# The down product of 1024 sample tokens as seven products over pairs of token tiles instead of eight

## The chip, the cores and the metric

One NeuronCore of a Trainium2 chip runs the whole program. The metric is device time in microseconds, from launch to the last output; runs of one kernel agree within about 0.3%. The trace of one profiled execution gives start, duration and wait of each instruction. Engines: TensorE (PE, with its weight loads as PEld), VectorE (DVE), ScalarE (ACT), GpSimd (POOL), SyncE (SP, which issues nearly all DMA transfers).

## What is computed

One layer of a diffusion transformer over 1024 sample tokens and 128 prompt tokens, in float32. The change touches only the last product, the down product of the feed-forward block:

```python
h = rmsnorm(x, P['g_pre_ffn'][l]) * (1.0 + sc2) + sh2
gt, up = jnp.split(h @ P['w_gate_up'][l], 2, axis=-1)
f = (jax.nn.silu(gt) * up) @ P['w_down'][l]        # (1152 x 2816) @ (2816 x 1024)
x = x + g2 * rmsnorm(f, P['g_post_ffn'][l])
```

## The kernel before

A float32 product is made of three PE passes: each operand is split into a high part (a copy by ACT into a rounded type, `copy`) and a low part (the difference, by DVE, `lo`), and `mm3` adds high x low, high x high and low x high. Every operand tile thus costs one ACT and one DVE instruction before PE can use it. `mm3` issues the two products with the high part of the stationary operand first.

The **gate and up stage** already uses seven products for eight: `VIS` lists 25 visits to the 22 hidden tiles g of 128 hidden units; each visit makes seven products (p = 0 to 6) for one or both chunks of tokens (c = 0: 640 tokens, c = 1: 512 tokens). Tokens of a tile of 128 are taken as two halves of 64. POOL makes the sums of weights (`weight_sums`), DVE combines the PSUM banks (`after`), and the hidden values `hf` go to HBM as `HB[tile, partition, j, token]`. The first three tiles g = 0, 1, 2 are visited for c = 0 alone and come back for c = 1 after g = 6, 10, 14. In the last visit c = 0 and c = 1 are done one after the other, so that loads for the next stage can begin between them.

The **down stage** has 18 runs `(n, t)`: two halves n of 512 output columns, nine token tiles t (tile 8 is the prompt). A run is 22 x 3 = 66 matmuls of 512 columns into one PSUM bank. Weights are loaded as 512 KB pieces (`load_d`, tile names raw_gu) and split into dw and gu tiles (`split_d`); the hidden tiles of a run are two halves of 11 (`load_h`, tile hr, 704 KB, two buffers; `split_h`, tile hd). In the second half the runs end with `post`: ACT squares the bank for the norm, DVE multiplies by the gain, POOL makes the reciprocal root (`rstd2`), DVE adds the residual `xr` twice, and SP stores the output tile `y`.

The order of the work on each engine is the order of the code (no scheduler moves anything). Each engine, SP included, takes its instructions in that order, and SP's are the issues of transfers: a transfer that waits, for a buffer or for data, is at the head of SP's queue, and what the code issues later comes behind it. ACT and DVE run ahead of PE as far as buffers and these orders allow; `post` of a run stands at j = 1 of the run after it.

Of the kernel before, what the change touches and what calls it, by code (L numbers as in the profile page):

```python
# [16 lines left out]
P = 128  # L17
D = 1024
# [3 lines left out]
NT = T // P  # L22
# [66 lines left out]
def _layout(inp):  # L89
    a = {k: np.asarray(v) for k, v in inp.items()}  # L90
    o = {}
# [15 lines left out]
    o["w_down"] = (a["w_down"][0].reshape(NJ // 2, 2, P, 2, 512).transpose(0, 3, 2, 1, 4)  # L107
                   .reshape(NJ, P, D))
# [44 lines left out]
def _body(tc, nc, A):  # L153
# [39 lines left out]
    ML = tc.dram_tile([D, T], F32, name="ML")  # L193
    X1 = tc.dram_tile([T, D], F32, name="X1")
    HB = tc.dram_tile([NT, P, NJ, P], F32, name="HB")
    H2B = tc.dram_tile([2, P, D], F32, name="H2B")
    GR = tc.dram_tile([2, 16, P], F32, name="GR")

# [1376 lines left out]

    dw, dstage = [], {}

    def load_d(i):  # L1580

        if i < NJ:
            r = (raw[1][:, 0], raw[1][:, 1], raw[0][:, 0])[i % 3]
            n, j = divmod(i, NJ // 2)
            dstage[i] = r
            SP.dma_start(r, A["w_down"][2 * j + n])

    def split_d(i):
        if i < 2 * NJ:
            r, w = dstage[i // 2][:, i % 2 * 512:i % 2 * 512 + 512], dw[i % len(dw)]  # L1590
            copy(ACT, w[:, 0], r)
            lo(w[:, 1], r, w[:, 0])
            if i % 2:
                load_d(i // 2 + 3)

    hid, hraw = {}, {}

    def load_h(t, i):

        r = hraw[t, i] = dp.tile([P, NJ // 2, P], F32, name=f"hr{t}{i}{len(hid)}", tag="hr", bufs=2)  # L1600
        SP.dma_start(r, HB[t, :, NJ // 2 * i:NJ // 2 * (i + 1)])

    def split_h(t, i):
        h = hid[t, i] = dp.tile([P, 2, NJ // 2, P], F32R, name=f"hd{t}{i}{len(hid)}", tag="hd", bufs=4)
        r = hraw.pop((t, i))
        copy(ACT, h[:, 0], r)
        lo(h[:, 1], r, h[:, 0])

    nprep = NS0
    extra = second_chunk()  # L1610
    H8 = 4
    for v, (g, cs) in enumerate(VIS):
        last = v == NV_ - 1
        for c_ in ([(c,) for c in cs] if last else [cs]):
            if last and c_ == (1,):
                avp.release()
                dp = pool("dp", side="right", reuse_waits="tile")
                load_h(0, 0)
                G2 = [dp.tile([P, D], F32, name="G2"), raw[0][:, 1]]
                fv = dp.tile([P, NT, 2], F32, name="fv")  # L1620
            for p in range(7):
                q = 7 * v + p
                while nprep <= q + LEADQ:
                    prep(nprep)
                    nprep += 1
                if q == 4:
                    op[0].release()
                    gb = pool("gb", space=PSUM, reuse_waits="tile")
                    banks += [4, 5]
                bs = [product(q, c) for c in c_]  # L1630
                if q in (H8, H8 + 1):
                    h2_turn(8, q - H8)
                    h2_mod(8, q - H8)
                if q == 13:
                    banks += [6, 7]
                after(q, c_, bs)
                if extra is not None and next(extra, 1):
                    extra = None
                if v == NV_ - 2 and p == 3:
                    load_d(0)  # L1640
                    load_d(1)
                if last and c_ == (0,):
                    if p == 0:
                        dw += [mo.tile([P, 2, 512], F32R, name=f"dw{i}", tag="tm" if i < 2 else "ou",
                                       bufs=2) for i in range(4)] + slots
                    if p == 3:
                        load_d(2)
                    if 1 <= p <= 4:
                        split_d(p - 1)
                elif last:  # L1650
                    if p == 1:
                        load_h(0, 1)
                    if p == 4:
                        split_h(0, 0)
                    if p > 0:
                        split_d(p + 3)
        if v == 2:
            assert extra is None

    fp.release()  # L1660
    dq = pool("dq", reuse_waits="tile")
    dw += [dq.tile([P, 2, 512], F32R, name=f"dw{i}") for i in range(len(dw), 24)]
    fg = [dq.tile([P, 512], F32, name=f"fg{t}") for t in range(NT)]
    xr = {}

    def load_x1(t):
        xr[t] = dp.tile([P, D], F32, name=f"xr{t}", tag="xr", bufs=2)
        SP.dma_start(xr[t], X1[t * P:(t + 1) * P])

    def post(t, n, b):  # L1670
        gt = G2[0 if t < 8 else 1][:, 512 * n:512 * n + 512]
        ACT.activation(t2, b, AF.Square, accum_out=fv[:, t, n:n + 1])  # L1672
        f = t3 if n else fg[t]
        DVE.tensor_tensor(f, b, gt, op=OP.mult)
        if n:
            rstd2(fv[:, t])
            x = xr[t].rearrange("p (n c) -> p n c", c=512)
            for i, y in enumerate((fg[t], t3)):
                DVE.scalar_tensor_tensor(x[:, i], y, fv[:, t, 0:1], x[:, i], op0=OP.mult, op1=OP.add)
                if t == 0:  # L1680
                    SP.dma_start(A["y"][t * P:(t + 1) * P, 512 * i:512 * i + 512], x[:, i])
            if t > 0:
                SP.dma_start(A["y"][t * P:(t + 1) * P], xr[t])

    runs = [(0, t) for t in range(NT)] + [(1, t) for t in reversed(range(NT))]
    done = None
    for i, (n, t) in enumerate(runs):
        nxt = None
        if n == 0 and t + 1 < NT:
            nxt = t + 1  # L1690
        elif n == 1 and 0 < t < NT - 1:
            nxt = t - 1
        b = bank(f"d{n}_{t}")
        for j in range(NJ):
            if i == 0 and j + 10 < NJ:
                split_d(j + 10)
            if j == 0:
                if nxt is not None and i:
                    load_h(nxt, 0)
                    load_h(nxt, 1)  # L1700
                if n:
                    load_x1(t)
            if i == 0 and j == 2:
                split_h(0, 1)
            if i == 0 and j in (6, 8):
                load_h(nxt, int(j > 6))
            if i == 0 and j == 11:
                grow(G2[0], 1, 0)
                grow(G2[1], 1, 1)
            if nxt is not None and j in ((14, 18) if i == 0 else (8, 14)):  # L1710
                split_h(nxt, int(j > 8 if i else j > 14))
            if j == 1 and done is not None:
                post(*done)
            if (n, t) == (0, 7) and j in (16, 18):
                split_d(NJ + (j - 16) // 2)
            h = hid[t, j // 11]
            w = dw[(NJ * n + j) % len(dw)]
            mm3(b, h[:, 0, j % 11], h[:, 1, j % 11], w[:, 0], w[:, 1], j == 0, j == NJ - 1)
            if (n, t) == (0, NT - 1) and j > 0:
                split_d(NJ + 2 + j - 1)  # L1720
        done = t, n, b
    post(*done)
    dp.release()
    mo.release()
    ring.release()
# [27 lines left out]
```

## Time and profile before

| what | value |
|---|---|
| median of 3 runs (lowest to highest) | 1435.22 us (1434.53 to 1440.06) |
| the profiled execution, its own time | 1430.3 us |
| its span, first to last instruction | 1428.5 us |
| its mean granted TensorE clock | 0.995 of full speed |
| PE, DVE, ACT, POOL busy, share of the span | 96%, 58%, 40%, 30% |

Busy shares are averages over stages that differ. PE's matmuls overlap in the pipeline, so that their listed durations (some 390 ns for 512 columns) are longer than the distance from one to the next. "SPq" rows are the issues of transfers by SP; a landing time runs from the issue to the end of the transfer.

### The profile page before, as it was taken

To read this page: it belongs to the slowest core of one execution; us is meant where nothing else is said; L and a number is where in the kernel's file an instruction comes from. 1 tells how busy PE (TensorE), PEld (TensorE's weight loads), DVE (VectorE), ACT (ScalarE), POOL (GpSimd) and SP (SyncE) were. 2 spreads that over 40 slices of the span, in tenths; PEclk is the share of its full clock that TensorE was granted. 3 is DMA by queue.
4 is the path that set the end of the run, shared out by engine and by line. 5 is a ranking of instruction groups with operands and counts; after the bars stand their busy time and mean duration, and the time that the engine had idled before them with its cause. 6 is when DMAs were issued, how large, how long until landed. Compare 5 with 4: busy or idle time off the path is not lost.

```text
span 1428.5 us, 22758 instructions
## 1 busy us (share of the span) xinstructions
PE 1375.9 (96%) x8918; PEld 1248.9 (87%) x8918; DVE 822.0 (58%) x1247; ACT 573.4 (40%) x1138; POOL 427.6 (30%) x426
## 2 busy tenths in 40 slices
PE   7899999998999999998999999999999989999998
PEld 6887799888889888887899999999999968888886
DVE  5724464564888843667866767667666653243232
ACT  6511136734888863555322323223222342142120
POOL 2301111222666662447634334333423100000000
PEclk9999999999999999999999999999999999999999
DMA  8558840147755335563222312222222472334541
GB/s 328 178 202 276 266 158 31 63 158 174 179 136 146 96 108 166 176 209 111 78 93 64 101 59 93 84 74 99 67 77 82 137 275 89 115 109 166 182 151 59
DMA packets 108326, 193.40 MB, mean 135 GB/s; under 512 B 7701, under 2 KB 77754, under 8 KB 104762
## 3 DMA queue, kind: packets, MB, share of 16 engines
q1 hardware_dynamic: 108074, 191.41, 41.7%
q8 instruction: 71, 1.16, 0.4%
q10 hardware_dynamic: 144, 0.52, 0.1%
q14 instruction: 37, 0.30, 0.1%
HBM read 146.67 MB, written 45.24 MB: 134 GB/s over the span
## 4 chain that ended last, share of the span: by engine, by line
PE 49%; DVE 2%; issue 1%; ACT 1%; DMA 1%; POOL 0%; DVEq 0%; POOLq 0%; SPq 0%; ACTq 0%
PE g L186 10%; PE g L184 10%; PE g L185 10%; PE d L186 6%; PE d L184 6%; PE d L185 6%; DVE gu L174 1%; DMA hr<-HB 1%; DVE av L174 0%; ACT gu L168 0%; DMA raw_gu<-in_w_down 0%; DVE u L1530 0%; DVE hf L1530 0%; DVE hd L174 0%; ACT av L168 0%
## 5 line engine op out<-in xcount | busy, mean ns | idle before, releaser
L186 PE MATMUL g<-av,gu 128*128 128x320 f32 (+1 forms) x1232 | 364.2, 296 | 7.7 <-DVE gu L174 7.3
L184 PE MATMUL g<-av,gu 128*128 128x320 f32 (+1 forms) x1232 | 364.3, 296 | 1.2 <-ACT av L168 0.8
L185 PE MATMUL g<-av,gu 128*128 128x320 f32 (+1 forms) x1232 | 363.1, 295 | 0.0
L186 PEld LDWEIGHTS g<-av,gu 128*128 128x128 f32 x1232 | 232.1, 188 | 10.3 <-DVE gu L174 10.2
L184 PEld LDWEIGHTS g<-av,gu 128*128 128x128 f32 x1232 | 231.9, 188 | 2.3 <-issue 1.4
L185 PEld LDWEIGHTS g<-av,gu 128*128 128x128 f32 x1232 | 232.2, 188 | 0.0
L174 DVE TENSOR_TENSOR gu<-raw_gu,gu 128x512 fp32r<-128x512 f32 x139 | 141.2, 1023 | 40.1 <-ACT gu L168 40.1
L184 PE MATMUL pu<-hl,w 128*128 128x384 f32 x336 | 123.0, 366 | 4.6 <-POOL hl L174 3.8
L186 PE MATMUL pu<-hh,w 128*128 128x384 f32 x336 | 113.1, 337 | 0.0
L185 PE MATMUL pu<-hh,w 128*128 128x384 f32 x336 | 113.1, 337 | 0.0
L184 PE MATMUL d<-dw,hd 128*128 128x512 f32 x270 | 106.7, 395 | 3.2 <-DVE dw L174 3.1
L186 PE MATMUL d<-dw,hd 128*128 128x512 f32 x270 | 106.4, 394 | 0.9 <-DVE hd L174 0.9
L185 PE MATMUL d<-dw,hd 128*128 128x512 f32 x270 | 106.4, 394 | 0.0
L1371 POOL TENSOR_TENSOR raw_gu<-raw_gu,t 128x512 f32<-128x512 f32 x25 | 33.2, 1329 | 233.4 <-DVE gu L174 233.4
L1530 DVE TENSOR_TENSOR u<-g,u 128x320 f32<-128x320 f32 (+1 forms) x176 | 77.5, 450 | 29.8 <-PE g L186 29.8
L940 PE MATMUL s<-ks,qs 128*128 128x384 f32 x384 | 91.0, 358 | 3.0 <-ACT p L953 1.5
L946 DVE TENSOR_REDUCE nm<-s 128x1 f32<-128x1152 f32 x64 | 86.6, 1353 | 9.4 <-PE s L940 9.2
L953 ACT ACTIVATE p<-s,nm 128x1152 f32<-128x1152 f32 x64 | 78.2, 1222 | 29.5 <-DVE nm L946 16.4
L1672 ACT ACTIVATE t<-d 128x512 f32<-128x512 f32 x18 | 10.7, 596 | 186.4 <-PE d L186 186.4
L168 ACT ACTIVATE gu<-raw_gu 128x512 fp32r<-128x512 f32 x139 | 83.4, 620 | 3.5 <-DMA raw_gu<-in_w_down 3.4
L1080 POOL TENSOR_SCALAR fv<-fv 128x1 f32<-128x1 f32 x9 | 2.7, 303 | 271.5 <-ACT t L1672 271.5
L184 PEld LDWEIGHTS pu<-hl,w 128*128 128x128 f32 x336 | 63.3, 189 | 21.7 <-issue 14.1
(276 smaller groups left out, 2867.4 us busy)
## 6 DMA issues: line engine op xcount, KB each, us to landing
raw_gu<-in_w_gu SPq DMA_DIRECT2D x25, 1024.0 KB, 4.8
hr<-HB SPq DMA_DIRECT2D x32, 704.0 KB, 5.0
wmb<-in_w_mod SPq DMA_DIRECT2D x32, 512.0 KB, 5.0
raw_gu<-in_w_down SPq DMA_DIRECT2D x22, 512.0 KB, 4.2
HB<-hf SPq DMA_DIRECT2D x18, 576.0 KB, 3.1
x<-in_x SPq DMA_DIRECT2D x18, 512.0 KB, 4.6
wm<-in_w_mod SPq DMA_DIRECT2D x16, 512.0 KB, 7.7
raw<-in_w_in_u SPq DMA_DIRECT2D x14, 512.0 KB, 7.7
```

Of the source, the lines that this page charges most:

```text
L168: ACT.activation(out, in_, AF.Copy)
L174: eng.tensor_tensor(out, x, hi.bitcast(F32), op=OP.subtract)
L184: PE.matmul(out, wh, xl, start=first, stop=False)
L185: PE.matmul(out, wh, xh, start=False, stop=False)
L186: PE.matmul(out, wl, xh, start=False, stop=last)
L940: PE.matmul(b[:, j, :CW], q[:, st_, m, i * P:(i + 1) * P], ks[:, m, j * CW:(j + 1) * CW], start=(st_ == 0), stop=(st_ == 1))
L946: DVE.tensor_reduce(nm, s, axis=AX.XY, op=OP.max, negate=True)
L953: ACT.activation(p.rearrange("p (n c) -> p n c", c=CW), s, AF.Exp, bias=nm, accum_out=ss)
L1080: POOL.tensor_scalar(v[:, 0:1], v[:, 0:1], v[:, 1:2], D * EPS, op0=OP.add, op1=OP.add)
L1371: POOL.tensor_tensor(b21, b21, t2, op=OP.subtract)
L1530: add = lambda out, x: DVE.tensor_tensor(out, b, x, op=OP.add)
L1672: ACT.activation(t2, b, AF.Square, accum_out=fv[:, t, n:n + 1])
```

## The change

The sample's eight token tiles are taken as four pairs r, tile 2r and tile 2r + 1; the 22 hidden tiles as two halves of 11; the output columns as two halves. That is a 2 x 2 by 2 x 2 block product, for which seven products p (`NDP`) stand instead of eight. A run `(p, r)` is now 11 x 3 = 33 matmuls; there are 7 x 4 runs for the pairs and 4 runs for the prompt tile (r = 4), 32 in all, in the order of p.

The sums of operands are made by POOL beside gate and up: `down_weight_sums` loads the weights of a hidden tile j and of j + 11, makes four sums and stores them to `WT` (one j per whole visit, from the first one on); `hidden_sums` loads the hidden tile j back from `HB`, takes tile j + 11 from `hf`, makes four sums and stores them to `HS` (in the visit after that of j + 11, and for the last j after the stage's end). The visits of g = 0, 1, 2 for c = 1 come after g = 5, 7, 9. Weights of a product are 11 tiles of 512 columns in 22 buffers, so that one product's are split while the product before it runs; `load_h` and `split_h` fetch one tile of 11 per run, and `load_h(k + 1)` stands at j = 1 of run k, behind `down_after` of run k - 1. `down_after` adds banks into the accumulators `acc`; an output tile is finished in each run of p = 5 and p = 6.

```diff
-        if g in (6, 10, 14):
-            VIS.append((g // 4 - 1, (1,)))
+        if g in (5, 7, 9):
+            VIS.append((g // 2 - 2, (1,)))
...
+    def down_weight_sums(j, step):
+        if step == 0:
+            TW[:] = [mo.tile([P, 2, 512], F32, name=f"tw{j}{i}", tag="tm", bufs=2) for i in range(2)]
+            for i in range(2):
+                SP.dma_start(TW[i].rearrange("p a c -> p (a c)"), A["w_down"][j, :, D * i:D * i + D])
+            return
+        b11, b12, b21, b22 = [TW[i][:, k] for i in range(2) for k in range(2)]
+        if step == 1:
+            POOL.tensor_tensor(b22, b22, b12, op=OP.subtract)
+            POOL.tensor_tensor(b12, b12, b11, op=OP.subtract)
+        else:
+            POOL.tensor_tensor(b11, b11, b22, op=OP.add)
+            POOL.tensor_tensor(b21, b21, b11, op=OP.subtract)
+            for i in range(2):
+                SP.dma_start(WT[j, :, D * i:D * i + D], TW[i].rearrange("p a c -> p (a c)"))
+    def hidden_sums(j, step):
+        if step == 0:
+            SA[:] = [mo.tile([P, 8, P], F32, name=f"sa{j}{i}", tag="ou", bufs=2) for i in range(2)]
+            SP.dma_start(SA[0], HB[0:8, :, j].rearrange("t p c -> p t c"))
+            return
...
+        if step == 1:
+            POOL.tensor_tensor(s1, a21, a22, op=OP.add)
+            POOL.tensor_tensor(a21, a11, a21, op=OP.subtract)
+        else:
+            POOL.tensor_tensor(a11, s1, a11, op=OP.subtract)
+            POOL.tensor_tensor(s4, a12, a11, op=OP.subtract)
+            for i in range(2):
+                SP.dma_start(HS[i][:, :, j].rearrange("t p c -> p t c"), SA[i])
+    WSRC = ((0, 0), (1, 0), (0, 2), (1, 3), (1, 1), (1, 2), (0, 3))
+    def hsrc(p, r):
...
+        return (HB[2 * r, :, k0], HS[0][2 * r], HB[2 * r, :, k1], HS[0][2 * r + 1], HS[1][r],
+                HB[2 * r + 1, :, k1], HS[1][4 + r])[p]
...
+            if j % 2 or j == NK - 1:
+                load_d(li + 4)
...
+            r = hraw[k] = dp.tile([P, NK, P], F32, name=f"hr{k}", tag="hr", bufs=2)
+            SP.dma_start(r, hsrc(*runs[k]))
...
+            h = hid[k] = dp.tile([P, 2, NK, P], F32R, name=f"hd{k}", tag="hd", bufs=3)
...
+    assert sums_d == NK and sums_h == NK - 1
+    hidden_sums(sums_h, 1)
+    hidden_sums(sums_h, 2)
...
+        elif p == 5:
+            add(c21, c21)
+            norm_half(2 * r + 1, 0, c21)
+            out_tile(2 * r + 1, c21, c22)
...
+    for k, (p, r) in enumerate(runs):
+        b = bank(f"d{p}_{r}")
+        for j in range(NK):
...
+            if j == 1:
+                if done is not None:
+                    down_after(*done)
+                if k > 0:
+                    load_h(k + 1)
+            if j == (5 if k else 7):
+                split_h(k + 1)
...
+            if j == 6 and (p == 5 or p == 6):
+                load_x1((2 * r + 1 if p == 5 else 2 * r) if r < 4 else 8)
+            if (11 * k + j) % 3 == 2 and (k or j > 7) and ndw < NK * (p + 2):
+                split_d(ndw)
+                ndw += 1
```

Three places show the order of instructions. First SP's queue where output tiles are finished; hr are the hidden loads (in before, `hr5018` and `hr5118` are the two halves of tile 5 for the run after next; now the number is that of the run), xr the residual, out_y the store. Before:

```order
L1668 DMA xr7_12691<-X1_70 128x1024
L1683 DMA out_y<-xr8_12616 128x1024
L1601 DMA hr5018_12773<-HB_71 128x1408
L1601 DMA hr5118_12775<-HB_71 128x1408
L1668 DMA xr6_12777<-X1_70 128x1024
L1683 DMA out_y<-xr7_12691 128x1024
```

Of the changed kernel, runs 24 to 26:

```order
L1757 DMA xr1_13163<-X1_70 128x1024
L1650 DMA raw_gu1_6640<-in_w_down 128x512
L1772 DMA out_y<-xr1_13163 128x1024
L1670 DMA hr25_13197<-HB_71 128x1408
L1757 DMA xr3_13221<-X1_70 128x1024
L1772 DMA out_y<-xr3_13221 128x1024
L1670 DMA hr26_13254<-HB_71 128x1408
```

Before, the store of tile 8 stands ahead of the halves for tile 5, two runs of 66 matmuls after the run that begins next. Now the store of the tile finished by run 23 stands ahead of the hidden tile for run 25, with one run of 33 matmuls between them.

Second DVE within the products. Names: hd is the hidden split, dw and gu the weight splits, fg and acc what is made of a finished bank d. Before, in the first half:

```order
L1674 TENSOR_TENSOR fg1_11821<-d0_1_11941,G2_11677 128x512
L174 TENSOR_TENSOR hd306_12051<-hr306_12021,hd306_12051 128x1408
L174 TENSOR_TENSOR hd317_12072<-hr316_12023,hd317_12072 128x1408
L1674 TENSOR_TENSOR fg2_11822<-d0_2_12020,G2_11677 128x512
L174 TENSOR_TENSOR hd408_12130<-hr408_12100,hd408_12130 128x1408
```

Of the changed kernel, in the third product (runs 9 to 12):

```order
L175 TENSOR_TENSOR hd10_12488<-hr10_12472,hd10_12488 128x1408
L175 TENSOR_TENSOR gu4_6637<-raw_gu0_5835,gu4_6637 128x512
L175 TENSOR_TENSOR gu5_6638<-raw_gu0_5835,gu5_6638 128x512
L175 TENSOR_TENSOR gu6_6639<-raw_gu0_5835,gu6_6639 128x512
L1777 TENSOR_TENSOR acc00_12019<-d2_0_12467,acc00_12019 128x512
L175 TENSOR_TENSOR dw15_12035<-raw_gu1_6640,dw15_12035 128x512
L175 TENSOR_TENSOR hd11_12540<-hr11_12524,hd11_12540 128x1408
L175 TENSOR_TENSOR dw16_12036<-raw_gu1_6640,dw16_12036 128x512
```

and SP's queue at the same place, where raw_gu are the weight loads, each of which waits for the split that empties its buffer (the two ahead of hr11 for gu4 and gu6, the one ahead of hr12 for dw16):

```order
L1670 DMA hr10_12472<-HB_71 128x1408
L1650 DMA raw_gu0_5835<-WT_74 128x2x512
L1650 DMA raw_gu0_5835<-WT_74 128x512
L1670 DMA hr11_12524<-HB_71 128x1408
L1650 DMA raw_gu1_6640<-WT_74 128x2x512
L1670 DMA hr12_12573<-HB_71 128x1408
```

Weight splits and their loads have come between the hidden splits and the hidden loads; before, the hidden loads of the first half stood one after the other.

Third SP's queue where gate and up end and the down stage begins (HS are the stores of the last hidden sums, G2 the gains). Before:

```order
L1586 DMA raw_gu1_6637<-in_w_down 128x1024 x2
L1601 DMA hr102_11868<-HB_71 128x1408
L1586 DMA raw_gu0_5832<-in_w_down 128x1024
L1601 DMA hr112_11881<-HB_71 128x1408
L1586 DMA raw_gu1_6637<-in_w_down 128x1024 x2
L1066 DMA G2_11677<-GR_73 128x1024
```

Of the changed kernel, with hr2 for the third run:

```order
L1556 DMA HB_71<-hf24_11790 128x4x128
L1616 DMA HS0_72<-sa100_11985 128x8x128
L1616 DMA HS1_73<-sa101_11986 128x8x128
L1650 DMA raw_gu1_6640<-WT_74 128x2x512 x2
L1069 DMA G20_12042<-GR_76 128x1024
L1069 DMA G21_12043<-GR_76 128x1024
L1650 DMA raw_gu0_5835<-WT_74 128x2x512
L1670 DMA hr2_12101<-HB_71 128x1408
```

Two stores that wait for POOL's sums now stand there, ahead of the weight loads, the gains and the hidden load for run 2.

## Rows read from the trace of the kernel before

**Rows 1.** Stretch, length; PE, PEld, DVE, ACT, POOL busy (instructions); clock, DMA share, GB/s.
```profile
1018.00:1081.00 63.00, 63.00 (x478) 63.00 (x477) 40.65 (x63) 17.53 (x33) 22.27 (x15) 1.00 0.23 77
1142.00:1163.00 21.00, 16.88 (x70) 12.48 (x70) 13.55 (x20) 11.32 (x18) 0.74 (x1) 1.00 0.79 265
1163.00:1293.00 130.00, 130.00 (x564) 105.42 (x562) 44.23 (x46) 37.82 (x55) 0.00 (x0) 1.00 0.41 140
1293.00:1422.00 129.00, 129.00 (x558) 104.29 (x556) 38.36 (x38) 23.28 (x30) 6.92 (x16) 1.00 0.37 129
```

**Rows 2.** Timeline of PE, first and last d matmul: start us, duration.
```profile
1141.93 0.39 PE L184 MATMUL d<-dw,hd 128*128 128x512 f32 x1
...
1421.66 0.40 PE L186 MATMUL d<-dw,hd 128*128 128x512 f32 x1
```

**Rows 3.** Timeline of SP's issues over one run of the second half.
```profile
1333.77 0.34 SPq L1683 DMA_DIRECT2D out_y<-xr  x1
1335.30 1.85 SPq L1601 DMA_DIRECT2D hr<-HB  x2
1337.21 0.42 SPq L1668 DMA_DIRECT2D xr<-X  x1
...
1349.03 0.34 SPq L1683 DMA_DIRECT2D out_y<-xr  x1
```

**Rows 4.** Waits of SP's queue, 1142 to 1428: total us, times, longest.
```profile
SPq L1683 <- DVE xr L1679: 94.9, 8, 14.7
```

**Rows 5.** Timeline of POOL and DVE in a whole visit of gate and up.
```profile
911.42 1.69 POOL L1354 TENSOR_TENSOR t<-t,raw_gu 128x512 f32<-128x512 f32 x1
911.88 1.78 DVE L174 TENSOR_TENSOR gu<-raw_gu,gu 128x512 fp32r<-128x512 f32 x1
...
916.55 0.68 DVE L174 TENSOR_TENSOR gu<-raw_gu,gu 128x512 fp32r<-128x512 f32 x1
```

**Rows 6.** Hidden tiles, all 32: durations in ns, first and last start, landing times.
```profile
L168 ACT ACTIVATE hd<-hr x32: 1365/1372/1387, 1138.4 to 1393.5; 128x1408 fp32r<-128x1408 f32 x32
L174 DVE TENSOR_TENSOR hd<-hr,hd x32: 1615/1620/1628, 1140.1 to 1396.3; 128x1408 fp32r<-128x1408 f32 x32
...
DMA to landing us min/median/max: 3.9/5.0/7.4
```

**Rows 7.** Two pairs of hidden loads, second half and first half.
```profile
L1601 SPq DMA_DIRECT2D hr<-HB x2: 319/320/320, 1335.3 to 1336.8; - x2
...
DMA to landing us min/median/max: 4.1/5.3/6.6
...
L1601 SPq DMA_DIRECT2D hr<-HB x2: 319/320/320, 1181.5 to 1183.1; - x2
...
DMA to landing us min/median/max: 4.0/4.8/5.7
```

**Rows 8.** Timeline of a run's end in the second half, ACT and DVE.
```profile
1330.56 0.60 ACT L1672 ACTIVATE t<-d 128x512 f32<-128x512 f32 x1 [12.04 <-PE d L186]
...
1331.28 0.69 DVE L1674 TENSOR_TENSOR t<-d,G 128x512 f32<-128x512 f32 x1 [9.73 <-ACT t L1672]
...
1333.00 0.74 DVE L1679 SCALAR_TENSOR_TENSOR xr<-t,fv,xr 128x512 f32<-128x512 f32 x1
```

**Rows 9.** Timeline at the end of gate and up: last hidden values and their store.
```profile
1144.80 0.43 DVE L1552 TENSOR_TENSOR hf<-hf,u 128x256 f32<-128x256 f32 x1
...
1145.30 0.38 SPq L1553 DMA_DIRECT2D HB<-hf  x1
```

**Rows 10.** Busy time by stretch, early and behind the last matmul; the clock is third last.
```profile
10.00:20.00 10.00, 6.59 (x44) 6.02 (x43) 6.20 (x11) 9.35 (x21) 5.45 (x12) 0.83 1.03 404
1426.00:1427.00 1.00, 0.00 (x0) 0.00 (x0) 0.00 (x0) 0.00 (x0) 0.00 (x0) 1.00 0.94 350
1427.00:1428.00 1.00, 0.00 (x0) 0.00 (x0) 0.00 (x0) 0.00 (x0) 0.00 (x0) 0.59 0.00 0
```

More of the change, by code (lines that the diff above doesn't have):

```diff
@@ L27 @@
 NJ = HID // P
+NK = NJ // 2
 NH = 4
@@ L195, in _body @@
     HB = tc.dram_tile([NT, P, NJ, P], F32, name="HB")
+    HS = [tc.dram_tile([8, P, NK, P], F32, name=f"HS{i}") for i in range(2)]
+    WT = tc.dram_tile([NK, P, 4 * 512], F32, name="WT")
     H2B = tc.dram_tile([2, P, D], F32, name="H2B")
@@ new lines, in hidden_sums @@
+    def hidden_sums(j, step):
[3 more added lines that the diff above has]
+            return
+        pair = lambda x: x[:, :8 * P].rearrange("p (r e c) -> p r e c", e=2, c=P)
+        flat = lambda x: x.rearrange("p t c -> p (t c)")
+        (a11, a21), (a12, a22) = [[pair(x)[:, :, e] for e in range(2)]
+                                  for x in (flat(SA[0]), TMP_H[0])]
+        s1, s4 = [SA[1][:, 4 * i:4 * i + 4] for i in range(2)]
+        if step == 1:
[6 more added lines that the diff above has]
+                SP.dma_start(HS[i][:, :, j].rearrange("t p c -> p t c"), SA[i])
@@ new lines, in _body @@
+    TW, SA, TMP_H = [], [], [None]
+    WSRC = ((0, 0), (1, 0), (0, 2), (1, 3), (1, 1), (1, 2), (0, 3))
+    NDP = len(WSRC)
+    def hsrc(p, r):
+        k0, k1 = slice(0, NK), slice(NK, NJ)
+        if r == 4:
+            return HB[8, :, k0 if p in (0, 4) else k1]
+        return (HB[2 * r, :, k0], HS[0][2 * r], HB[2 * r, :, k1], HS[0][2 * r + 1], HS[1][r],
+                HB[2 * r + 1, :, k1], HS[1][4 + r])[p]
+    runs = []
+    for p in range(NDP):
+        rs = list(range(4))
+        if p % 2 == 0:
+            rs = [4] + rs if p == 6 else rs + [4]
+        runs += [(p, r) for r in rs]
@@ L1596, in _body, with load_h @@
     hid, hraw = {}, {}
[L1598 to L1607, printed above, removed]
+    def load_h(k):
+        if k < NR:
+            r = hraw[k] = dp.tile([P, NK, P], F32, name=f"hr{k}", tag="hr", bufs=2)
+            SP.dma_start(r, hsrc(*runs[k]))
@@ L1609, in _body, with split_h @@
+    def split_h(k):
+        if k < NR:
+            h = hid[k] = dp.tile([P, 2, NK, P], F32R, name=f"hd{k}", tag="hd", bufs=3)
+            r = hraw.pop(k)
+            copy(ACT, h[:, 0], r)
+            lo(h[:, 1], r, h[:, 0])
     nprep = NS0
@@ L1617, in _body @@
                 dp = pool("dp", side="right", reuse_waits="tile")
-                load_h(0, 0)
-                G2 = [dp.tile([P, D], F32, name="G2"), raw[0][:, 1]]
-                fv = dp.tile([P, NT, 2], F32, name="fv")
+                load_h(0)
+                load_h(1)
+                dw += [dp.tile([P, 2, 512], F32R, name=f"dw{i}") for i in range(2, 8)] + slots
             for p in range(7):
@@ L1638, in _body @@
                     extra = None
+                if sums_h is not None and p in (2, 3) and not (last and c_ == (1,)):
+                    hidden_sums(sums_h, p - 1)
+                    if p == 3:
+                        sums_h = None
+                if whole and not last and v >= 3 and sums_d < NK and p in (0, 4, 5):
+                    down_weight_sums(sums_d, max(p - 3, 0))
+                    sums_d += p == 5
+                if g >= NK and whole and p == 5 and (not last or c_ == (1,)):
+                    hidden_sums(g - NK, 0)
+                if g >= NK and whole and p == 6 and (not last or c_ == (1,)):
+                    sums_h, TMP_H[0] = g - NK, TMP["hf"][1]
                 if v == NV_ - 2 and p == 3:
@@ L1643, in _body @@
                     if p == 0:
-                        dw += [mo.tile([P, 2, 512], F32R, name=f"dw{i}", tag="tm" if i < 2 else "ou",
-                                       bufs=2) for i in range(4)] + slots
+                        dw += [mo.tile([P, 2, 512], F32R, name=f"dw{i}", tag="tm", bufs=2)
+                               for i in range(2)]
                     if p == 3:
                         load_d(2)
-                    if 1 <= p <= 4:
-                        split_d(p - 1)
+                        load_d(3)
@@ L1660, in _body @@
+    hidden_sums(sums_h, 1)
+    hidden_sums(sums_h, 2)
     fp.release()
     dq = pool("dq", reuse_waits="tile")
-    dw += [dq.tile([P, 2, 512], F32R, name=f"dw{i}") for i in range(len(dw), 24)]
-    fg = [dq.tile([P, 512], F32, name=f"fg{t}") for t in range(NT)]
+    acc = {(r, n): dq.tile([P, 512], F32, name=f"acc{r}{n}") for r in range(4) for n in range(4)}
+    dw += [dq.tile([P, 2, 512], F32R, name=f"dw{i}") for i in range(15, 20)]
+    dw += [mo.tile([P, 2, 512], F32R, name=f"dw{i}", tag="ou", bufs=2) for i in (20, 21)]
@@ L1664, in _body @@
+    G2 = [dq.tile([P, D], F32, name=f"G2{r}") for r in range(2)]
+    fv = dq.tile([P, NT, 2], F32, name="fv")
+    jk = dp.tile([P, 512], F32, name="fj")
+    acc[4, 0], acc[4, 1] = t2, t3
     xr = {}
     def load_x1(t):
-        xr[t] = dp.tile([P, D], F32, name=f"xr{t}", tag="xr", bufs=2)
+        xr[t] = dq.tile([P, D], F32, name=f"xr{t}", tag="xr", bufs=2)
         SP.dma_start(xr[t], X1[t * P:(t + 1) * P])
[L1670 to L1683, printed above, removed]
@@ L1685, in _body, with norm_half @@
-    runs = [(0, t) for t in range(NT)] + [(1, t) for t in reversed(range(NT))]
-    done = None
[L1687 to L1707, printed above, removed]
+    def norm_half(t, n, a, eng=DVE):
+        ACT.activation(jk, a, AF.Square, accum_out=fv[:, t, n:n + 1])
+        eng.tensor_tensor(a, a, G2[0 if t < 8 else 1][:, 512 * n:512 * n + 512], op=OP.mult)
@@ new lines, in out_tile, with down_after, add @@
+    def out_tile(t, a0, a1):
+        rstd2(fv[:, t])
+        x = xr[t].rearrange("p (n c) -> p n c", c=512)
+        for i, y in enumerate((a0, a1)):
+            DVE.scalar_tensor_tensor(x[:, i], y, fv[:, t, 0:1], x[:, i], op0=OP.mult, op1=OP.add)
+            if t == 6:
+                SP.dma_start(A["y"][t * P:(t + 1) * P, 512 * i:512 * i + 512], x[:, i])
+        if t != 6:
+            SP.dma_start(A["y"][t * P:(t + 1) * P], xr[t])
+    def down_after(p, r, b):
+        def add(out, x):
+            DVE.tensor_tensor(out, b, x, op=OP.add)
+        if r == 4:
+            x, y = acc[4, 0], acc[4, 1]
+            if p == 0:
+                copy(ACT, x, b)
+            elif p == 2:
+                add(y, x)
+                norm_half(8, 0, y, POOL)
+            elif p == 4:
+                add(x, x)
+            else:
+                add(x, x)
+                norm_half(8, 1, x)
+                out_tile(8, y, x)
+            return
+        c11, c12, c21, c22 = [acc[r, n] for n in range(4)]
+        if p == 0:
+            copy(ACT, c11, b)
+        elif p == 1:
+            add(c12, c11)
+        elif p == 2:
+            add(c11, c11)
+            norm_half(2 * r, 0, c11, POOL)
+        elif p == 3:
+            add(c21, c12)
+        elif p == 4:
+            add(c22, c21)
+            add(c12, c12)
+            norm_half(2 * r + 1, 1, c22, POOL)
+        elif p == 5:
+            add(c21, c21)
+            norm_half(2 * r + 1, 0, c21)
+            out_tile(2 * r + 1, c21, c22)
+        else:
+            add(c12, c12)
+            norm_half(2 * r, 1, c12)
+            out_tile(2 * r, c11, c12)
@@ L1709, in _body @@
                 grow(G2[1], 1, 1)
[L1710 to L1722, printed above, removed]
+            if j == 6 and (p == 5 or p == 6):
+                load_x1((2 * r + 1 if p == 5 else 2 * r) if r < 4 else 8)
+            if (11 * k + j) % 3 == 2 and (k or j > 7) and ndw < NK * (p + 2):
+                split_d(ndw)
+                ndw += 1
+            w = dw[(NK * p + j) % (2 * NK)]
+            h = hid[k]
+            mm3(b, h[:, 0, j], h[:, 1, j], w[:, 0], w[:, 1], j == 0, j == NK - 1)
@@ L1723, in _body @@
+        done = p, r, b
+    assert ndw >= NK * NDP
+    down_after(*done)
     dp.release()
```

43 lines of the change are left out of this document (26 added, 17 removed).

## The prediction

> **What bounds the kernel now.** Read first the table by stretch. In the gate and up stage (first row of [rows 1]) TensorE (PE) is busy all 63 us, DVE 40.65, POOL 22.27. In the down stage PE is full again except in the first 21 us (the other rows of [rows 1]), and DVE and ACT have room. So PE sets the time. The down stage runs from the first d matmul at 1141.93 to the end of the last at 1422.06, 280.1 us [rows 2]. The y stores leave one per run of 66 matmuls, 15.26 us apart (first and last row of [rows 3]), so a matmul of 512 columns takes 0.2312 us. 1188 of them are 274.7 us: 5.4 us are lost, all at the start.
>
> Then read SP's queue, because every load is issued there in program order. In one run SP issues the y store, waits until the hidden loads' buffers come free, issues two hidden loads, and only then, 0.06 us behind them, the load of xr [rows 3]. SP spent 94.9 us standing at y stores, until DVE had the output [rows 4]. Now that costs nothing: the hidden tile behind a y store is needed two runs, 30 us, later.
>
> **What is removed.** The four pairs need 7 x 33 matmuls each instead of 8 x 33, so 4 x 33 = 132 fewer; the prompt tile keeps its 132. 132 x 0.2312 = **-30.5 us**, on PE's own path. Run 0 now needs only the first eleven hidden tiles, which lie in memory early, so the 5.4 us lost at the start can go: **-5.4 us**. 32 runs of 33 matmuls, 7.63 us each, replace 18 of 66.
>
> **Beside gate and up.** 88 POOL sums of 512 columns are added, four to a whole visit (eight in two visits). Such a sum took 1.69 us beside DVE, and a DVE split that ran beside it 1.78 instead of 0.68 [rows 5]. A whole visit is about 22 us; POOL is at 35% and DVE at 65% (first row of [rows 1]). Four sums bring POOL 7 us and DVE up to 4 x 1.1 = 4.4 us: 14.5 + 4.4 = 19 of 22. PE covers that; only in the two visits with eight sums is there none left. I take **+1 us** (0 to 4). The stores and loads of the sums, about 38 MB, go through DMA engines that are busy 23% of that stretch.
>
> **The chain that the shorter runs expose.** A hidden tile has to be issued, land, be copied by ACT (1.37 us) and subtracted by DVE (1.62 us) [rows 6]; with 0.15 us of handing over that is 3.15 us after landing. PE needs DVE's half at its third matmul, 0.47 us into a run. The landing time decides. In each of two pairs the later load is the slower one [rows 7]. The load 1.5 us behind the y store [rows 3] landed in 4.1 us; its neighbour, behind that load and with xr right behind itself, in 6.6; the later one of the pair without xr, 1.6 us behind the other, in 5.7; all 32 lie between 3.9 and 7.4, median 5.0 [rows 6]. In the new code a 512 KB transfer is issued only 0.4 us ahead of most hidden loads, so they are nearest to the 5.7 row. I take **5.5 us**, ends 3.9 and 7.4.
>
> The Trainium skill (DMA: Bandwidth & Descriptors, "Anatomy of one DMA") fits a transfer as about 2.0 us plus its bytes at 436 GB/s, for another issue path; that is an estimate of 3.7 us for 704 KB and 4.5 with 512 KB right ahead. The trace is slower than that in both cases, and I go by it.
>
> *Last two products.* Runs 23 to 30 end in a finished tile. On SP the y store of run k-1 stands ahead of the hidden load for run k+1. At a run's end the row of before takes 0.1 + 3.2 us from the last matmul to the y store [rows 3, 8]; now DVE's addition (0.69) comes first, so 4.0. The load goes out at 4.35, lands at 9.85, is ready at 13.0, so run k+1 can start 12.5 us after run k-1's end, but run k lasts 7.63. The wait is 4.9 us, and since the run after it then has its load early enough, it falls on every second run: loads 25 to 31 give four waits, **+19.6 us** (13 at 3.9, 27 at 7.4).
>
> *Products 1 to 4.* During the first runs of a product the eleven weights of the next are split, some of them after the hidden split on DVE. The weight load that waits for such a split stands on SP ahead of the next hidden load. So one hidden split waits for the one before: n x 0.68 + 0.4 (two issues) + landing + 3.15. Three such links follow each other in each product, with n = 2, 3, 2 in products 1 and 3 and 3, 1, 2 in products 2 and 4. That is 4.8 + 1.2 + 16.5 + 9.45 = 31.9 us, or 31.2, against 22.9 of three runs. The free runs at the product's end build a lead of about 4 us (hidden split done some 4 us into a run). Left are 5.0 and 4.3 us per product, **+18.6 us** for four (0 at 3.9, 41 at 7.4).
>
> *Handover.* The last hidden sums begin when hf is ready, 3.3 us after the first d matmul [rows 9], and take four POOL sums, 5.8 us at 1.45 each. Their two stores stand on SP ahead of three weight loads, two G2 loads and the hidden load for run 2. From the first store at 7.7 us that is 7 x 512 + 704 KB, 4.39 MB. The handover moved 265 GB/s at a DMA share of 0.79 (second row of [rows 1]), which is 335 if full; at 300 the load lands 14.6 us later, at 22.3, is ready at 25.5, and run 2 starts at 25.0 instead of 15.3: 9.8 us (2.8 without any queueing). Three links with n = 1 follow, 9.73 against 7.63, 6.3 us; the last 2.1 of these come back as lead in product 1. **+14 us** (4 to 22).
>
> *End.* One addition more ahead of the last output, **+0.7**.
>
> **Sum.** -30.5 - 5.4 + 1 + 14 + 18.6 + 19.6 + 0.7 = **+18.0 us**. The profiled execution took 1430.3 us, so its like is 1448.3; the runs shown have a median of 1435.2, 5 us above it, and there the sum gives **1453 us**. Of 1435, 0.5% (7 us) is about what a measurement tells from no change.
>
> **Rivals.** *The loads land fast, and it ends faster.* The DMA engines are busy 41% and 37% in the down stage [rows 1], and a load that is not crowded lands in about 4 us [rows 7]. The mechanism has one number, the landing time: at 3.9 the sum is -35.9 + 1 + 4 + 0 + 13.2 + 0.7 = -17 us, 1418. Between that and +18 at 5.5 the slope is 22 us per microsecond; it is even at 4.7 us and faster by 0.5% below 4.4. For it speaks the 4.1 row, against it that the transfer ahead is 0.4 us away and not 1.5, and that the stage moves more in less time: 20.2 MB of weights instead of 11.5, beside the same 23 MB of hidden tiles. The page's estimate of 4.5 us would give about -4 us by this line. Chance 0.12, and 0.13 for a landing between 4.4 and 5.0, which is no measurable change.
>
> *The clock falls in the waits.* Early in the kernel, with PE busy for 6.59 of 10 us, the granted clock averaged 0.83, which is 3.4 us at half speed, 1.2 instead of 2.4 GHz; at the end it was full until 1427 and fell in the next microsecond, 5 us behind the last matmul [rows 10]. The new waits are 3 to 10 us. If each of about nine costs 3.4 us at half speed, 1.7 us is lost each: +15, 1468. [...] The Trainium skill (TensorE: Matmul & The Clock Gate, "HAM oscillation") says that gaps for transfers bring the array back to half rate each time; here only rows 10 show it. Chance 0.2, with landings over 6.5 us.
>
> *DVE becomes the bound beside gate and up.* If POOL's sums slowed DVE past PE in all visits, up to 88 x 1.1 us would be added; DVE's 35% of room speaks against it. A third of that, 32 us, gives 1485. Chance 0.05.
>
> The forecast itself, landings of 5.0 to 6.5 us, has 0.5. The range reaches from a landing just above 4.2 us, 1426, to waits with a slow clock, 1476. Faster 0.13, the same 0.15, slower 0.72.
>
> **What the new profile would show.** Right: 1056 d matmuls, 0.2312 us apart when they flow; gate and up still full; PE waits released by DVE's hd, some 5 us at every second run in the last two products, 2 to 5 us once or twice per product before, and about 10 us ahead of run 2; SP waiting at y stores and weight loads. Wrong: waits for hd of under 30 us in all, or hidden loads that land in 4 us, or gaps in gate and up. The prediction would be most wrong if SP's queue were ahead of these waits and the loads were there in time: then most of the 36 us is gained.

## The result and the profile after

The changed kernel takes 1491.39 us (median of 4 runs, 1485.83 to 1495.75) against 1434.88 us (4 runs, 1432.62 to 1440.06) beside it: the ratio is 1.0387 [1.0346, 1.0429], 56.5 us slower. The forecast was 18 us slower; 1491 lies above its range.

The profiled execution is at 1495.75 us, 65.4 above the profiled one of before (1430.3); both stand a few us from their medians, on opposite sides. First the page of the changed kernel: its span, and the 40 slices of PE's busy time and of its granted clock.

```profile
span 1493.8 us, 22869 instructions
...
PE   7899999998999999998999999999999799888775
...
PEclk8999999999999999999999999999999899999878
```

A slice is 37.3 us. Until the handover (the 32nd slice, 1158 to 1195 us) PE is busy for nine tenths or more, but for four slices with 7 or 8; from there it thins out to the end, most of all in the last three slices, where the clock is lower too. That points at the down stage. Now the table by stretch: two stretches late in gate and up (the second answers to the first row of [rows 1]), the handover in two pieces, part of product 1, and the last two products in two pieces.

```profile
955.00:1018.00 63.00, 63.00 (x479) 63.00 (x478) 41.66 (x64) 16.10 (x30) 45.25 (x31) 1.00 0.61 191
1018.00:1081.00 63.00, 63.00 (x478) 63.00 (x477) 38.85 (x63) 17.09 (x32) 37.55 (x26) 1.00 0.50 154
...
1155.00:1178.00 23.00, 11.66 (x45) 7.86 (x43) 10.08 (x8) 5.32 (x10) 6.47 (x4) 0.84 0.78 261
1178.00:1209.00 31.00, 30.95 (x130) 25.17 (x131) 13.81 (x16) 12.68 (x18) 0.00 (x0) 0.96 0.47 164
1209.00:1247.00 38.00, 32.35 (x119) 24.56 (x118) 15.61 (x19) 10.61 (x14) 0.00 (x0) 0.87 0.42 137
1376.00:1429.00 53.00, 39.47 (x135) 29.30 (x134) 21.93 (x29) 10.66 (x18) 5.42 (x8) 0.82 0.36 125
1429.00:1486.00 57.00, 44.64 (x153) 33.32 (x151) 17.34 (x20) 8.40 (x12) 5.41 (x8) 0.84 0.40 143
```

Beside gate and up, POOL is at 38 to 45 us of 63 instead of 22, the DMA share has more than doubled, and PE is still busy for all 63. In the last two products no engine is full: PE is at 74% and 78%, DVE at 41% and 30%, and the DMA engines have 0.36 and 0.40 of their time filled, where it was 0.37 [rows 1]. When nothing is full, a chain of waits sets the time. The next view is of PE's waits in the down stage, by who ended them (total us, times, longest), and under it the same for SP's queue.

```profile
PE d L185 <- ACT hd L169: 44.7, 14, 8.5
PE d L187 <- DVE hd L175: 13.1, 17, 1.2
PE d L185 <- DVE gu L175: 1.3, 2, 0.7
```

```profile
SPq L1650 <- DVE dw L175: 120.1, 21, 12.9
SPq L1772 <- DVE xr L1768: 51.6, 8, 8.1
SPq L1650 <- DVE gu L175: 47.4, 6, 13.5
SPq L1772 <- DMA xr<-X: 40.4, 8, 5.8
```

All of PE's waits are for splits, 57.8 of 59.1 us for the hidden ones: 44.7 us ahead of a run's first matmul, until ACT's copy was there, and 13.1 ahead of its third, until DVE's difference was. SP, which has to issue the hidden loads, stood 167.5 us at weight loads (L1650, until a split emptied their buffer) and 92.0 us at y stores (L1772, until the output was there). In before the y stores alone took as much [rows 4], at no cost.

A table from the starts and ends of matmuls places the 65.3 us by which the two spans differ (the last instructions of both programs as the end):

| part | before | after | difference |
|---|---|---|---|
| start of the span to first g matmul | 639.1 | 645.4 | +6.3 |
| first g matmul to first d matmul | 502.8 | 502.8 | 0.0 |
| first d matmul to end of last | 280.1 | 337.9 | +57.8 |
| from there to the end of the span | 6.5 | 7.7 | +1.2 |

32 runs of 7.63 us are 244.1, so the down stage lost 93.8 us to waits. Cut where ACT or DVE begins to read the last bank of a product, product 0 lost 15.3 (53.4 instead of 38.15), products 1 to 4 lost 34.3 (171.6 instead of 137.3), and the last two products 44.2 (112.8 instead of 68.7). The forecast had 16.1, 16.5 (18.6 less the lead of 2.1) and 19.6.

The timeline over one run of the last two products shows the loop (start us, duration; in brackets idle time before, and what ended it):

```profile
1428.43 0.34 SPq L1772 DMA_DIRECT2D out_y<-xr  x1
1428.86 0.38 SPq L1670 DMA_DIRECT2D hr<-HS  x1
1429.29 0.78 SPq L1757 DMA_DIRECT2D xr<-X  x1
...
1433.72 0.39 PE L187 MATMUL d<-gu,hd 128*128 128x512 f32 x1
...
1434.76 1.38 ACT L169 ACTIVATE hd<-hr 128x1408 fp32r<-128x1408 f32 x1 [9.34 <-DMA hr<-HS]
1436.16 1.63 DVE L175 TENSOR_TENSOR hd<-hr,hd 128x1408 fp32r<-128x1408 f32 x1 [7.76 <-ACT hd L169]
1436.19 0.50 PE L185 MATMUL d<-dw,hd 128*128 128x512 f32 x1 [2.08 <-ACT hd L169]
1437.71 0.68 DVE L1777 TENSOR_TENSOR t<-d,t 128x512 f32<-128x512 f32 x1
...
1440.78 1.42 DVE L1768 SCALAR_TENSOR_TENSOR xr<-t,fv,xr 128x512 f32<-128x512 f32 x2 [0.84 <-POOL fv L1084]
1442.22 0.34 SPq L1772 DMA_DIRECT2D out_y<-xr  x1
```

Follow it from the top. SP can issue the y store of run k-1 at 1428.43 and, right behind it, the hidden load for run k+1. That lands after 5.8 us and is copied by ACT and split by DVE until 1437.8. PE had ended run k at 1434.1. But the addition for run k (L1777) stands behind the split for run k+1 in DVE's order, so it starts at 1437.71, and the output of run k leaves at 1442.22, not 4 but 8.1 us after PE's end. Only then may SP issue the load for run k+2. The loop passes once through every run: 13.8 us here, while PE works 7.63. The eight y stores 1385.48 to 1481.55 are 13.72 us apart on average.

### The profile page after: what moved, and what is told of

Read it like the earlier page. It is cut to its first block, busy times and chain, and to the rows that moved or that the text cites. A ratio compares the mean times of both kernels' runs of the same rounds, so it can differ in the third digit from the quotient of the medians.

```text
span 1493.8 us, 22869 instructions
## 1 busy us (share of the span) xinstructions
PE 1382.7 (93%) x8786; PEld 1244.4 (83%) x8786; DVE 876.5 (59%) x1302; ACT 593.8 (40%) x1176; POOL 581.6 (39%) x523
## 4 chain that ended last, share of the span: by engine, by line
PE 36%; DMA 8%; DVE 6%; ACT 3%; issue 2%; POOL 1%; SPq 1%; ACTq 0%; DVEq 0%; POOLq 0%
PE g L187 10%; PE g L185 10%; PE g L186 10%; DMA hr<-HB 4%; DMA hr<-HS 4%; PE d L187 2%; PE d L185 2%; PE d L186 2%; ACT hd L169 2%; DVE hd L175 2%; DVE gu L175 1%; DVE dw L175 1%; DVE xr L1768 1%; DVE acc L1777 0%; POOL fv L1083 0%
## 5 line engine op out<-in xcount | busy, mean ns | idle before, releaser
L175 DVE TENSOR_TENSOR gu<-raw_gu,gu 128x512 fp32r<-128x512 f32 x149 | 163.2, 1107 | 36.8 <-ACT gu L169 36.8
L175 DVE TENSOR_TENSOR hd<-hr,hd 128x1408 fp32r<-128x1408 f32 x32 | 53.1, 1658 | 145.0 <-ACT hd L169 145.0
L185 PE MATMUL d<-dw,hd 128*128 128x512 f32 x244 | 104.3, 428 | 32.3 <-ACT hd L169 32.2
L187 PE MATMUL d<-dw,hd 128*128 128x512 f32 x244 | 104.3, 428 | 10.8 <-DVE hd L175 10.8
L169 ACT ACTIVATE hd<-hr 128x1408 fp32r<-128x1408 f32 x32 | 44.0, 1374 | 155.8 <-DMA hr<-HS 76.4
L186 PE MATMUL d<-dw,hd 128*128 128x512 f32 x244 | 102.4, 419 | 0.0
L185 PEld LDWEIGHTS d<-dw,hd 128*128 128x128 f32 x244 | 50.9, 209 | 47.8 <-ACT hd L169 37.0
L956 ACT ACTIVATE p<-s,nm 128x1152 f32<-128x1152 f32 x64 | 78.2, 1222 | 29.2 <-DVE nm L949 16.2
L169 ACT ACTIVATE gu<-raw_gu 128x512 fp32r<-128x512 f32 x149 | 88.9, 619 | 0.0
L1762 POOL TENSOR_TENSOR acc<-acc,G 128x512 f32<-128x512 f32 x8 | 10.3, 1291 | 185.6 <-ACT fj L1761 185.6
```

The costliest lines, as they stand in the source:

```text
L956: ACT.activation(p.rearrange("p (n c) -> p n c", c=CW), s, AF.Exp, bias=nm, accum_out=ss)
L1762: eng.tensor_tensor(a, a, G2[0 if t < 8 else 1][:, 512 * n:512 * n + 512], op=OP.mult)
```

## The experiments

Theory A: the hidden loads are late because of where they stand on SP, behind transfers that wait (y stores, weight loads), and in the last two products the wait comes round in every run. Its rivals: the lower clock, crowded DMA engines that make every load slow, and the residual load that the y store waits for. Runs 1 to 4 share a kernel before of 1433.39 us (7 runs), runs 5 to 7 one of 1433.95 us (9 runs).

**1. Hidden loads issued earlier in the last two products.** The load for run k+3 goes out right behind the split for run k+1, which empties its buffer, in place of standing behind the y store of run k+1. Buffers and work are the same.

```diff
-                if k > 0:
+                if k > 0 and not EARLY(k + 1):
                     load_h(k + 1)
             if j == (5 if k else 7):
                 split_h(k + 1)
+                if EARLY(k + 3):
+                    load_h(k + 3)
```

Here EARLY(k) is k >= 25.

> Only in the last two products (runs 25 to 31) the hidden load of run k is issued right behind the split that empties its buffer (that of run k-2), ahead of the y stores and residual loads. Theory A (a loop through SP and DVE: y store, hidden load, hidden split, addition, y store, 13.7 us per run): the loop is cut, about 40 of the 44 us that PE loses there come back, the time falls to about 1452 us. Theory B (the transfers themselves are slow, wherever they stand): the loads land just as late, 1480 to 1491 us. The forecast's own two-run chain put 20 us there: 1472 us if that was all.

Measured: 1451.15 us (1449.66 to 1452.86), ratio to before 1.0128 [1.0102, 1.0153], 40.2 us below the changed kernel. The last two products took 75.9 us instead of 112.8, products 0 to 4 what they took without the edit, to within 3 us. Three of SP's y stores there:

```profile
1399.06 0.34 SPq L1775 DMA_DIRECT2D out_y<-xr  x1
...
1408.26 0.34 SPq L1775 DMA_DIRECT2D out_y<-xr  x1
...
1416.96 0.34 SPq L1775 DMA_DIRECT2D out_y<-xr  x1
```

The first six are 9 us apart instead of 13.7. The place of the load on SP's queue made the loop.

**2. The same edit in products 1 to 4** (runs 5 to 22) and the two runs behind them, with EARLY(k) for 5 <= k < 25.

> The same early issue for runs 5 to 24 only (products 1 to 4), where weight loads that wait for a DVE split stand ahead of the hidden loads. Theory A (hidden split, weight split, weight load, hidden load, hidden split as one chain): 30 of the 34 us lost there come back, about 1461 us. Theory B (landing times of 5.5 to 9 us set by the DMA engines, not by the order): 1485 to 1491 us.

Measured: 1456.87 us (1452.84 to 1466.05), ratio 1.0180 [1.0138, 1.0222], 34.5 us below the changed kernel. Products 1 to 4 took 136.2 us, no longer than 18 runs of PE (137.3); the last two stayed at 113.7. So here too the loss was the order on SP, all of it.

**3. The same edit everywhere**, EARLY(k) for k >= 2 (`load_h(2)` right behind the split for run 0).

> The early issue for all runs from 2 on, so also ahead of the last hidden sums' stores. Theory A: most of the 94 us that PE loses in the down stage come back (10 to 15 stay at the beginning and in loads that crowd each other), 1405 to 1412 us, faster than the kernel before. Theory B: 1470 us or more.

Measured: 1410.31 us (1407.32 to 1415.66), ratio 0.9850 [0.9820, 0.9880], 81.1 us below the changed kernel and faster than before. Product 0 took 42.6 us instead of 53.4. By medians 6.4 us (81.1 - 40.2 - 34.5) come from there, by the stage times of the profiles some 11; it was not tried by itself. PE's waits in the down stage:

```profile
PE d L187 <- DVE hd L175: 6.6, 7, 1.3
PE d L185 <- ACT hd L169: 0.9, 1, 0.9
```

7.5 us are left of 59. The first six y stores stay 8.9 us apart on average, 1.3 above PE's 7.63, and SP's issues show why:

```profile
1345.66 0.34 SPq L1775 DMA_DIRECT2D out_y<-xr  x1
1347.80 0.32 SPq L1670 DMA_DIRECT2D hr<-HS  x1
1348.17 0.42 SPq L1760 DMA_DIRECT2D xr<-X  x1
1354.77 0.34 SPq L1775 DMA_DIRECT2D out_y<-xr  x1
```

The residual is asked for only 6.6 us ahead of the store that waits for it.

**4. PE filled up in the last two products.** 16 more matmuls per run, on weights that are split already, into a bank that nobody reads; the output stays the same. They keep PE busy while it would wait, so that the clock need not fall.

```diff
+        if p > 4:
+            wd = dw[NK * p % (2 * NK)]
+            z = bank(f"z{p}_{r}")
+            for i in range(16):
+                PE.matmul(z, wd[:, 0, :P], wd[:, 0], start=(i == 0), stop=(i == 15))
         b = bank(f"d{p}_{r}")
```

> In the last two products 16 more matmuls of 512 columns stand ahead of each run (3.7 us per run), on weights that are long split, into a bank that nobody reads; the results are unchanged. They fill PE's waits, so that its clock stays up. Theory A (PE is not in the loop, 7.6 + 3.7 = 11.3 us is less than its 13.7): 1489 to 1494 us, and a granted clock near 1.00 in that stretch. Theory C (the clock at half speed, granted 0.82 and 0.84 there, costs part of the 44 us): 1473 to 1483 us.

Measured: 1495.73 us (1490.38 to 1497.36), ratio 1.0436 [1.0407, 1.0465], 4.3 us above the changed kernel and 1.7 above the range of theory A. Its rows for the last two products, and the first and the eighth y store:

```profile
1376.00:1429.00 53.00, 48.69 (x202) 38.31 (x201) 18.92 (x26) 10.68 (x18) 5.44 (x8) 0.96 0.34 119
1429.00:1486.00 57.00, 52.71 (x214) 41.48 (x213) 18.43 (x22) 8.41 (x12) 5.43 (x8) 0.95 0.38 136
```

```profile
1387.20 0.34 SPq L1772 DMA_DIRECT2D out_y<-xr  x1
...
1483.23 0.34 SPq L1772 DMA_DIRECT2D out_y<-xr  x1
```

The granted clock was 0.96 and 0.95 instead of 0.82 and 0.84, and the kernel no faster; over seven intervals its y stores were 13.72 us apart, as without the edit. The two products took 116.4 us, 3.6 more, all of it ahead of the first y store, where one block of 16 stands in front of a run that did not wait. The clock was lower because PE waited, and it cost nothing in that stretch, since PE is not in the loop.

**5. Experiment 3 with the residual asked for earlier**, at j = 0, ahead of the y store of the run before, instead of at j = 6.

```diff
+            if j == 0 and (p == 5 or p == 6):
+                load_x1((2 * r + 1 if p == 5 else 2 * r) if r < 4 else 8)
...
-            if j == 6 and (p == 5 or p == 6):
-                load_x1((2 * r + 1 if p == 5 else 2 * r) if r < 4 else 8)
```

> The early hidden loads for all runs, and each residual load issued at the start of its run, ahead of the y store of the run before (it stood behind it). In the kernel with the early hidden loads alone the y stores of the last two products are still 9.0 us apart for five runs of 7.63, each 6.5 us behind its residual load. If that is a loop of store, residual load and addition, 6 to 10 us come back, 1400 to 1404 us; if the residual load is not in the loop, 1408 to 1412 us.

Measured: 1404.73 us (5 runs, 1401.43 to 1405.83), ratio 0.9791 [0.9769, 0.9812]: 29.2 us below the kernel before, 86.7 below the changed one, 0.7 above the range for a loop through the residual. By stretch, the handover, products 1 to 4 and the last two:

```profile
1146.00:1190.00 44.00, 40.19 (x166) 31.67 (x166) 25.39 (x27) 17.18 (x25) 8.32 (x5) 0.96 0.80 273
1190.00:1326.00 136.00, 136.00 (x595) 111.28 (x594) 72.62 (x83) 56.92 (x86) 11.68 (x9) 1.00 0.55 179
1326.00:1394.00 68.00, 68.00 (x298) 55.62 (x297) 41.80 (x52) 18.35 (x30) 10.83 (x16) 1.00 0.59 210
```

From 1190 on PE is full again at full clock, and the last y stores are 7.48 us apart (1361.55 to 1391.47). The down stage takes 248.6 us, 4.5 above its matmuls, lost at the handover.

**6. Weight loads cut to a quarter.** The loads of products 1 to 6 fetch 128 of their 512 columns, and the rest keeps old contents, so the down product isn't the reference's. The order on every queue is that of the changed kernel; only the bytes ahead of the hidden loads are fewer.

```diff
-            SP.dma_start(r[:, :512 * m].rearrange("p (j c) -> p j c", c=512),
-                         (WT if src else A["w_down"])[2 * li:2 * li + m, :, 512 * c:512 * c + 512]
+            n = 128 if p else 512
+            SP.dma_start(r[:, :512 * m].rearrange("p (j c) -> p j c", c=512)[:, :, :n],
+                         (WT if src else A["w_down"])[2 * li:2 * li + m, :, 512 * c:512 * c + n]
```

> The changed kernel, in which the weight loads of products 1 to 6 fetch only the first 128 of 512 columns (the other three quarters of each tile keep what was there, so the down product is not the reference's). Order, waits and numbers of instructions stay. If the hidden loads land late because the weight loads issued right ahead of them move 512 KB each (landings of 5.5 to 9 us where the forecast had 5.5), the landings in products 1 to 4 fall to some 5 us and the time by 12 to 22 us, to 1469 to 1479; if they are late for another reason (the rows' address pattern, the order alone), 1487 to 1495.

Measured: 1463.32 us (1461.73 to 1465.45), ratio 1.0204 [1.0179, 1.0229], 28.1 us below the changed kernel, more than expected. Products 1 to 4 took 143.9 us instead of 171.6, the last two 112.9, as without the edit. The landing of the hidden loads in products 1 to 4, first of the changed kernel, then of this one:

```profile
DMA to landing us min/median/max: 3.9/7.2/9.3
```

```profile
DMA to landing us min/median/max: 3.9/4.4/6.2
```

So in products 1 to 4 the landing was late because of the weights ahead, and most of the loss went with it (the weights land sooner too, which was not told apart); in the last two products, where little stands ahead, bytes don't matter and the order does.

**7. The changed kernel with only the residual moved**, the diff of experiment 5 without that of 3.

> The changed kernel, with only the residual loads moved to the start of their run, ahead of the y store of the run before. SP's waits name the residual load for 40 us in the last two products. If it is what holds the y stores there, 25 to 40 us come back (1451 to 1466 us). If the loop runs through the hidden load and the hidden split, and the residual is merely the first of two things waited for, the time is 1482 to 1493 us, a little less at most because the hidden load has one transfer less behind it.

Measured: 1489.52 us (1486.83 to 1492.10), ratio 1.0392 [1.0362, 1.0421], 1.9 us below the changed kernel. The y stores are 13.3 us apart (1379.94 to 1472.83, seven intervals). The 40.4 us that the view of waits puts down to the residual at L1772 were thus not in the loop: the output would have come no earlier. The edit is worth 5.6 us once the loop is gone (experiment 5 against 3, by medians).

## Why the forecast was right in sign and too small

The sign and the broad mechanism held: 132 matmuls are gone, and late hidden tiles cost more than that. One step of the mechanism, in the last two products, failed, and one term was mis-sized. By its own steps:

- **Matmuls and the old start stall, -35.9.** Right for the matmuls: 32 runs at 7.63 us are what the stage takes when nothing waits; experiment 5 comes within 4.5 us of it. The stall at the start did not go: runs 0 and 1 lost 4.5 us, most of it to waits for their own hidden and weight splits (counted under the handover below).
- **Beside gate and up, +1.** Measured 0.0 (502.8 us both). The rival in which DVE becomes the bound did not happen: in seven stretches of 63 us from 703 to 1144 DVE was busy 38.9 to 49.1 us of 63.
- **Handover, +14 (16.1 ahead of the lead).** 15.3, but near in part by luck. The load for run 2 was issued behind the two HS stores, three weight loads and two G2 loads as foreseen, and PE's wait ahead of run 2 was 8.46 us (forecast 9.8). The three links behind it, 6.3 us, did not appear: runs 3 and 4 began without a wait. In their place runs 0 and 1 lost 4.5 us and run 2 itself 2.5, at a granted clock of 0.79.
- **Products 1 to 4, +18.6.** 34.3: the term that was mis-sized. That a chain through SP's order makes the loss was right, since cutting it (experiment 2) gives all of it back. The landing was taken as 5.5 us and its median was 7.2, almost the upper end. SP is held at the first of two weight loads; when DVE has split, both go out, and the hidden loads follow them at once:

```profile
1226.15 1.62 DVE L175 TENSOR_TENSOR hd<-hr,hd 128x1408 fp32r<-128x1408 f32 x1 [7.78 <-ACT hd L169]
1227.70 1.28 DVE L175 TENSOR_TENSOR gu<-raw_gu,gu 128x512 fp32r<-128x512 f32 x2
1228.41 1.64 SPq L1650 DMA_DIRECT2D raw_gu<-WT  x2
1230.11 0.93 SPq L1670 DMA_DIRECT2D hr<-HB  x2
...
1239.68 1.63 DVE L175 TENSOR_TENSOR hd<-hr,hd 128x1408 fp32r<-128x1408 f32 x1 [10.10 <-ACT hd L169]
```

  These two hidden loads landed in 8.1 and 9.3 us, and the splits are 13.5 us apart. The forecast chose the 5.7 row [rows 7], with one transfer ahead of the load; the six loads here that went out right behind two of 512 KB landed in 6.4 to 8.1 us. Twelve links of 1.7 us more make 39 us of the 18.6, or 37 less the handover's lead, against 34.3. That this fits so well is partly luck. The chain that ended last (what released what, followed back from the end of the program) runs through nine hidden loads in these products, of 5.5 to 8.1 us, 6.8 on average, not through twelve of 7.2, and it also runs through PE in runs 9, 13 and 22, just after a wait. Here is run 9 on that chain (start us, us, what):

```profile
1230.11 8.06 DMA hr<-HB
1238.27 1.39 ACT hd L169
1239.68 1.64 DVE hd L175
...
1242.16 0.43 PE d L185
...
1250.20 0.23 PE d L186
...
1250.69 0.70 DVE acc L1777
```

  Its first matmuls come 0.43 us apart instead of 0.23 (ten such distances in runs 9 and 13, eight in run 22), which makes some 2 us a run, 5 to 6 of the 34.3 (an estimate, and the most that it can be).

- **The last two products, +19.6.** 44.2: the step that failed. The sentence was "On SP the y store of run k-1 stands ahead of the hidden load for run k+1", with that store 4.0 us behind PE's end of run k-1. It counted DVE's addition, but as ready when PE is. In the code `split_h(k + 1)` stands at j = 5 of run k and `down_after` of run k at j = 1 of run k+1, so the addition waits for a hidden tile that itself waits for the y store of the run before. The chain through two runs, with a wait on every second run, is a loop through each run: 13.7 us, 6.1 lost per run. The landing in these products was 5.2 us in the median, so the size taken for it was right there.
- **End, +0.7.** +1.2.
- **Not in the sum, +6.3** in the profiled execution: gate and up began at 645.4 instead of 639.1. In the experiments, with the same code there, it began between 640.1 and 643.0. Most of it arises early: the matmuls into `mod` end at 54.0 us instead of 49.2, in the experiments at 49.3 to 53.0; why they vary was not studied.

Against the sum of 18.0 the profiled spans differ by 65.3, 47.3 more: 17.8 from products 1 to 4, 24.6 from the last two, 6.3 from the start and -1.4 from the other terms. The medians differ by 56.5, since the profiled execution of before lies 4.6 us below its median and that of after 4.4 above.

**The signs.** PE's waits for hidden tiles and SP's waits at y stores and weight loads came as foreseen, but in the last two products on every run, 25 to 31, and three quarters of PE's wait ended with ACT's copy instead of DVE's hd.

**The rivals.** That the loads land in 4 us did not happen, but experiment 6 shows the rule behind it: at 4.4 us products 1 to 4 lose 7 us instead of 34. The clock did fall in the waits (0.82 and 0.84 in the last two products); PE's matmuls there came 0.427 us apart after a wait (the 1.2 GHz level) and 0.227 when the run had flowed for some time (2.4 GHz). The Trainium skill (TensorE: Matmul & The Clock Gate, "HAM oscillation") says that gaps for transfers bring the array back to half rate, and these rows agree; but experiment 4 raised the clock in the last two products and gained nothing. PE's waits add up to 59 us and the loss to 93.8; most of the difference is matmuls at the lower clock beside the wait for the next tile. In products 0 to 4 the rival was not tried apart, and the chain that ended last says that it cost something there: it runs through the slow matmuls of runs 2, 9, 13 and 22, together some 7 us at most (an estimate: 35 distances of 0.43 us instead of 0.23), about half of the 15 that the rival was given. These waits are those for the late loads, and in experiment 2 the whole loss of products 1 to 4 went with the loads' place.

## What to carry to other kernels

When the work between two loads gets shorter, write out for each in-order queue what stands ahead of the load and what that waits for, and follow every wait back, through the compute engines' own order, until it reaches a load again: if it closes within one step, the loop and not the engine sets the time. Issue a load at the point in the program where its buffer comes free, ahead of stores and loads that wait for other work. Here that edit, at no cost in memory or work, turned 1.0387 into 0.9850, and with the residual load moved the same way into 0.9791.

## What was not expected of the hardware

- A 704 KB load lands in 3.9 us at the least, in 5.2 (median) right behind one y store of 512 KB, and in 8.1 us behind two loads of 512 KB whose issue began 1.7 us ahead (9.3 for the load right behind that one), with the DMA engines busy 42% of that stretch: the mean share says nothing about a load behind a burst.
- 88 more sums by POOL and a DMA share more than twice as high beside gate and up did not change PE's 502.8 us.
- In the last two products the clock of 0.82 and 0.84 and that of 0.96 and 0.95 gave the same distance of y stores, 13.72 us, with 16 more matmuls per run at the higher clock.
